# Gate/up weight sums of a seven-product block scheme: made once in DRAM by accumulating DMAs instead of on the chip for every use

## The chip, the cores and the metric

The kernel runs on one core of a Trainium2 chip. A core has a matrix engine (TensorE, PE in the profile), a vector engine (VectorE, DVE), a scalar engine (ScalarE, ACT), a general engine (GpSimd, POOL) and an engine that only issues transfers here (SyncE, SP). Each runs its own list of instructions in order and waits on semaphores that the others, or transfers, raise. Sixteen DMA engines move data between DRAM and the on-chip memory SBUF; PSUM is the memory of eight banks into which TensorE accumulates. The metric is the time of one execution on the device in microseconds.

## The reference

One layer of a decoder: 2048 tokens of width 1024, all float32.

```python
xn = rms_norm(h, mix_norm_w[l])
proj = jnp.einsum('bsd,de->bse', xn, w_in[l])        # 1024 -> 3072: q, f, i, g, lru_x, lru_gate
o_hg = hgrn2_mix(q, f_logit, i_v, g, lb_all[l], hg_norm_w[l])   # gated linear recurrence, 4 heads
o_lru = rglru_mix(lru_x, lru_gate, conv_w[l], ...)              # convolution, gates, linear recurrence
h = h + jnp.einsum('bse,ed->bsd', mixed, w_out[l])
hn = rms_norm(h, ffn_norm_w[l])
gate, up = jnp.split(jnp.einsum('bsd,df->bsf', hn, w_gate_up[l]), 2, axis=-1)   # 1024 -> 2 x 2816
h = h + jnp.einsum('bsf,fd->bsd', jax.nn.silu(gate) * up, w_down[l])
return rms_norm(h, final_norm_w)
```

## The kernel before

**Precision and halves.** Each float32 operand of a large matmul is split into a rounded part `hi` (a cast on ScalarE, L207 or L163) and the remainder `lo` (a subtraction on VectorE, L208 or L164). One product is then three matmuls: hi by hi, lo by hi, hi by lo. The tokens are worked in two halves of 1024, each in two chunks of 512. Both halves go through the projections, the mixers and the output projection first; then come gate/up and down for half 0, then gate/up and down for half 1.

**Start of the program.** For half 0 the first chunk of x is normalised and transposed on the chip (`norm_first`). The second chunk comes already transposed: `xk` (L482) loads one of eight tiles of 128 features, VectorE multiplies it by the norm weight and by a row of inverse norms (L483) that GpSimd and TensorE made (`ss_x`, `dg`, `tpb`, L475 and L476), and it is split into `xn`. The value projection `pv` (L246 to L248) of the four token tiles of chunk 0 comes first, then that of chunk 1, tile by tile of the contraction. After that come eight pairs of feature projections, `pa` and `pb` (L234 to L236), each for both chunks, with the mixers' steps between. Weights arrive as `raw_in` of 512 KB (L161) in three buffers.

**GpSimd's part in the mixers.** GpSimd copies the last three columns of each convolution input into `hist` (L389), which VectorE reads for the next chunk (L387), and raises sums of squares to the power -1/2 in `oss` (L379), which VectorE then multiplies with (L380).

**Gate/up.** Two tiles of 128 weight columns (a11, a12 and a21, a22, by halves of the contraction) and two chunks of tokens (b11 to b22) form a 2 by 2 block product, which seven products P1 to P7 give instead of eight. One such quad is 7 x 12 matmuls of 512 columns; there are 22 quads for each half. `Sums` loads a quad's weights in two DMAs (`raw`), makes the four sums S1 to S4 on VectorE and splits seven operands of 512 columns. The sums of the activations (`act_a` to `act_g`) are made once for each half. In `ffn_up` the products go into four PSUM banks, where P2, P3 and P4 add onto P1, P5 and P7, and five additions on VectorE fold them.

**What sets the order.** The program is written in order of use, but a scheduler decides when it is built where each instruction stands in its engine's list; it lets one overtake another where data and buffers allow. DMAs of one queue share eight completion semaphores in turn: each waits until the one eight places ahead in its queue has landed. SyncE issues every DMA of the kernel before.

Of the kernel before, what the change touches and what calls it, by code (L numbers as in the profile page):

```python
# [8 lines left out]
F32 = mybir.dt.float32  # L9
# [26 lines left out]
def hybrid_layer(ctx: ExitStack, tc: tile.TileContext, x, x_t, norm_w, cols, w_in, gate_w, w_out, w_gu, w_down, out):  # L36
# [467 lines left out]
    def acts(src, nm, direct):  # L504
        ops = {}
        held = []

        def put(name, k, p):
            split([ops[name][s][:, k, :] for s in range(2)], p)

        pages = {}

        def open_(names):
            for name in names:
                ops[name] = [block(f"act_{LET[name]}{s}_{nm}") for s in range(2)]


        def early(k):
            if k == 0:
                open_(("p1", "p5"))  # L520
            b11, b12 = (xin(f"{t}{k}_{nm}") for t in ("b11e_", "b12e_"))
# [3 lines left out]
            tt_(b12, b12, b11, SUB_)  # L525
            put("p5", k, b12)

        def load(k):
            if k == 0:
                open_(("p1", "p5", "p6", "p7", "p2", "p3", "p4") if direct else ("p6", "p7", "p2"))  # L530
            b11, b12 = (xin(f"{t}{k}_{nm}") for t in ("b11_", "b12_"))
            b21, b22 = ((late if direct else page)(f"{t}{k}_{nm}") for t in ("b21_", "b22_"))
            for p, n, c in ((b11, 0, 0), (b12, 0, 1), (b22, 1, 1), (b21, 1, 0)):
                nc.sync.dma_start(out=p, in_=src[n][k, :, c * CW : (c + 1) * CW])
            pages[k] = b11, b12, b21, b22

        def one(k):
            b11, b12, b21, b22 = pages[k]
            if direct:
                put("p1", k, b11)  # L540
            tt_(b11, b12, b11, SUB_)
            if direct:
                put("p5", k, b11)

        def two(k):
            b11, b12, b21, b22 = pages[k]
            tt_(b11, b22, b11, SUB_)
            tt_(b12, b22, b12, SUB_)
            put("p2", k, b21)
            put("p6", k, b11)  # L550
            tt_(b21, b21, b11, SUB_)
            put("p7", k, b12)
            if direct:
                put("p3", k, b22)
                put("p4", k, b21)
            held.append((b22, b21))

        def rest(i):
            name = ("p3", "p4")[i]
# [12 lines left out]
    ORDER = ("p1", "p5", "p6", "p7", "p2", "p3", "p4")  # L572


    class Sums:
        def __init__(self, src, nm):
            self.src, self.nm, self.op, self.raw, self.done = src, nm, {}, [None, None], set()

        def load(self, i):
            r = rawt(f"raw{i}_{self.nm}", (P, 2, CW))  # L580
            nc.sync.dma_start(out=r, in_=self.src[:, :, i * CW : (i + 1) * CW].rearrange("u p k -> p u k"))
            self.raw[i] = r

        def make(self, i):
            (a11, a21), (a12, a22) = ([r[:, u, :] for u in range(2)] if r is not None else (None, None) for r in self.raw)
            nm, name = self.nm, ORDER[i]
            if name == "p1":
                x = a11
            elif name == "p5":
                self.s1 = x = late("s1" + nm)  # L590
                tt_(x, a21, a22, ADD)
            elif name == "p6":
                self.s2 = x = late("s2" + nm)
                tt_(x, self.s1, a11, SUB_)
            elif name == "p7":
                x = late("s3" + nm)
                tt_(x, a11, a21, SUB_)
            elif name == "p2":
                x = a12
            elif name == "p3":  # L600
                x = late("s4" + nm)
                tt_(x, a12, self.s2, SUB_)
            else:
                x = a22
            w = wslot(f"wgu_{LET[name]}_{nm}", (P, 2, CW))
            split([w[:, s, :] for s in range(2)], x)
            self.op[name] = w

    def product(ps, w, b, first):
        for k in range(4):  # L610
            ks = slice(k * P, (k + 1) * P)
            hi, lo = b[0][:, k, :], b[1][:, k, :]
            for n, (s, x) in enumerate(((0, hi), (1, hi), (0, lo))):
                nc.tensor.matmul(  # L614
                    ps, lhsT=w[:, s, ks], rhs=x, start=first and k + n == 0, stop=k == 3 and n == 2, skip_group_check=not first
                )
# [5 lines left out]
    def sums(q):  # L622
        if q < len(quads) and q not in made:
            half, j, m = quads[q]
            f0 = m * NF + 2 * j
            made[q] = Sums(w_gu[f0 : f0 + 2], f"{half}_{j}_{m}")
        return made.get(q)

    def sums_start(q):
        s = sums(q)  # L630
        s.load(0)
        s.load(1)

    def ffn_up(half, bops, between=()):
        between = list(between)
        q0 = half * 2 * NPAIR
        for q in range(q0, q0 + 2 * NPAIR):
            _, j, m = quads[q]
            nm = f"{half}_{j}_{m}"
            s, nxt, nn = sums(q), sums(q + 1), sums(q + 2)  # L640
# [3 lines left out]
            end = q == q0 + 2 * NPAIR - 1 and half == 0  # L644
            for i, name in enumerate(ORDER):
                if q == q0 and i not in s.done:
                    s.make(i)
                product(dst[name], s.op.pop(name), bops[name], i < 4)
                if name == "p1":
                    e1 = page("e1" + nm)  # L650
                    nc.scalar.copy(out=e1, in_=b1)
                elif name == "p5":
                    e5 = page("e5" + nm)
                    nc.scalar.copy(out=e5, in_=b3)
                elif name == "p6":
                    u2 = page("u2" + nm)
                    tt_(u2, e1, b2, ADD)
                elif name == "p7":
                    u3 = page("u3" + nm)
                    tt_(u3, u2, b4, ADD)  # L660
                    tt_(e5, u3, e5, ADD)
                    if m == 0:
                        nc.scalar.activation(out=e5, in_=e5, func=AF.Silu)
                        sg22 = e5
                    else:
                        tt_(e5, e5, sg22, MUL)
                        a22 = e5
                elif name == "p2":
                    if m == 0:
                        sg11 = page("sg11" + nm)  # L670
                        nc.scalar.activation(out=sg11, in_=b1, func=AF.Silu)
                    else:
                        tt_(sg11, sg11, b1, MUL)
                        a11 = sg11
                elif name == "p3":
                    tt_(e1, u2, b3, ADD)
                    if m == 0:
                        nc.scalar.activation(out=e1, in_=e1, func=AF.Silu)
                        sg12 = e1
                    else:  # L680
                        tt_(e1, e1, sg12, MUL)
                        a21 = e1
                else:
                    tt_(u2, u2, b4, ADD)
                    if m == 0:
                        nc.scalar.activation(out=u2, in_=u2, func=AF.Silu)
                        sg21 = u2
                    else:
                        tt_(u2, u2, sg21, MUL)
                        store(half, j, a11, u2, a21, a22)  # L690
                if nxt is not None and not end:
                    nxt.make(i)
                    nxt.done.add(i)
                if between:
                    between.pop(0)()
                if nn is not None and i in (0, 4) and quads[q + 2][0] == half:
                    nn.load(i // 4)
            made.pop(q)


# [236 lines left out]
    for half in range(2):  # L937
# [36 lines left out]
        for s in range(8):  # L974
# [4 lines left out]
            for c in range(NC):  # L979
# [13 lines left out]
                pend.append(nxt)  # L993
        wg = ws.take(4)
# [76 lines left out]
        else:  # L1071
            first = sums(0)
            for i in range(1, 7):
                if i in (3, 5):
                    last.pop(0)()
                first.make(i)
                first.done.add(i)
            sums(1).load(0)
            sums(1).load(1)


    for half in range(2):
        ffn_up(half, bops[half], later if half == 0 else ())
        hp = residual(half)
        if half == 0:
# [5 lines left out]
            def first(i):  # L1091
                if i == 0:
                    sums_start(q)
                sums(q).make(i)
                sums(q).done.add(i)

            for c in range(NC):
                down_plain(0, c, range(16, NF), hp, extra, [lambda i=i: first(i) for i in range(7)] if c == 1 else ())
            fin.clear()
            sums(q + 1).load(0)  # L1100
            sums(q + 1).load(1)
# [7 lines left out]
def _layout(i):  # L1109
# [10 lines left out]
    def by_cols(w):  # L1120
        n = w.shape[1] // P
        return w.reshape(KT, P, n, P).transpose(2, 1, 0, 3).reshape(n, P, D)

# [14 lines left out]
    for m, t in enumerate((a["lru_wa"][0], a["lru_wx"][0])):  # L1138
# [11 lines left out]
        "w_gu": by_cols(a["w_gate_up"][0]),  # L1150
# [21 lines left out]
```

## Time and profile before

Three runs took 2129.33, 2132.01 and 2132.49 us. One execution was profiled.

| | us |
|---|---|
| median of the runs | 2132.01 |
| the profiled execution (its span) | 2131.1 |
| TensorE busy | 2101.2 (99%) |
| VectorE busy | 1493.1 (70%) |
| ScalarE busy | 1010.2 (47%) |
| GpSimd busy | 82.2 (4%) |
| DMA, mean over the span | 123 GB/s |

A group of instructions is told as line, engine, operation, what is written from what, count, busy us, mean ns of one, and the idle time of its engine just before, with what ended it. In a timeline a row begins with the start and the length in us. Numbers of buffers are left out of names. The mean of a pipelined matmul (0.39 us) is its latency; the distance from one to the next is shorter and is read from counts.

### The profile page before, as it was taken

The page shows a single profiled execution, that of the slowest core. Times are in us where ns is not written, and L with a number is a line of the kernel's source. Part 1 is how long each engine was busy: PE and PEld are TensorE (multiplying, and loading weights), DVE is VectorE, ACT ScalarE, POOL GpSimd, SP SyncE. Part 2 cuts the span into 40 slices and gives each one's busy share as a digit, 9 for nine tenths or more (in the row PEclk, how much of TensorE's full clock was granted, in tenths as well). Part 3 has the DMA queues.
Part 4 walks back from the last instruction along what each step waited for, and adds up shares of the span by engine and source line. Part 5 has one row for each costly group of instructions (what it writes and reads, how often), then busy time and mean ns, then how long its engine had stood idle before and what let it go on. Part 6 is the DMA issues. An engine that isn't in the chain of part 4 may idle for free.

```text
span 2131.1 us, 26161 instructions
## 1 busy us (share of the span) xinstructions
PE 2101.2 (99%) x9704; PEld 1735.7 (81%) x9704; DVE 1493.1 (70%) x2415; ACT 1010.2 (47%) x1647; POOL 82.2 (4%) x130
## 2 busy tenths in 40 slices
PE   8999999999999999999999999999999999999998
PEld 6887888888878888788888888888888888888887
DVE  6577664645776566877667669878867667669787
ACT  5577764535777644533333334335433333334333
POOL 2000001100000000000000000000000000000000
PEclk9999999999999999999999999999999999999999
DMA  6111104852111058433323257346423223257424
GB/s 216 61 40 40 40 20 160 282 162 69 31 39 40 20 174 260 156 112 99 106 93 129 89 187 253 109 136 205 143 94 119 95 90 123 94 206 252 156 88 143
DMA packets 138420, 262.84 MB, mean 123 GB/s; under 512 B 11186, under 2 KB 27570, under 8 KB 138292
## 3 DMA queue, kind: packets, MB, share of 16 engines
q1 hardware_dynamic: 138292, 261.17, 36.5%
q8 instruction: 76, 1.25, 0.2%
q14 instruction: 52, 0.43, 0.1%
HBM read 197.95 MB, written 63.18 MB: 123 GB/s over the span
## 4 chain that ended last, share of the span: by engine, by line
PE 83%; ACT 6%; DVE 5%; DMA 3%; issue 2%; SPq 0%; POOL 0%; DVEq 0%; POOLq 0%; ACTq 0%
PE quad_e L614 11%; PE quad_g L614 11%; PE quad_a L614 11%; PE pda L885 10%; PE pdb L885 6%; PE quad_f L614 5%; PE poh L246 2%; PE poh L247 2%; PE poh L248 2%; PE pb L236 2%; PE pb L234 2%; PE pb L235 2%; PE pa L234 1%; PE pa L235 1%; PE pg L248 1%
## 5 line engine op out<-in xcount | busy, mean ns | idle before, releaser
L614 PE MATMUL quad_f<-act_f,wgu_f 128*128 128x512 f32 x528 | 127.4, 389 | 1.8 <-DVE h L1050 1.7
L614 PE MATMUL quad_a<-act_a,wgu_a 128*128 128x512 f32 x528 | 127.5, 389 | 0.0
L614 PE MATMUL quad_g<-act_d,wgu_d 128*128 128x512 f32 x528 | 127.0, 389 | 0.2 <-DVE u L498 0.2
L614 PE MATMUL quad_g<-act_g,wgu_g 128*128 128x512 f32 x528 | 127.1, 390 | 0.0
L614 PE MATMUL quad_a<-act_b,wgu_b 128*128 128x512 f32 x528 | 127.1, 389 | 0.0
L614 PE MATMUL quad_e<-act_e,wgu_e 128*128 128x512 f32 x528 | 127.0, 389 | 0.0
L614 PE MATMUL quad_e<-act_c,wgu_c 128*128 128x512 f32 x528 | 126.9, 389 | 0.0
L614 PEld LDWEIGHTS quad_f<-act_f,wgu_f 128*128 128x128 f32 x528 | 99.0, 188 | 23.1 <-ACT act_g L207 2.1
L498 DVE TENSOR_TENSOR u<-u,quad_g 128x512 f32<-128x512 f32 x88 | 60.5, 687 | 80.9 <-PE quad_g L614 80.9
L614 PEld LDWEIGHTS quad_g<-act_d,wgu_d 128*128 128x128 f32 x528 | 99.0, 188 | 21.1 <-DVE u L498 0.6
L614 PEld LDWEIGHTS quad_e<-act_c,wgu_c 128*128 128x128 f32 x528 | 99.1, 188 | 20.6
L614 PEld LDWEIGHTS quad_g<-act_g,wgu_g 128*128 128x128 f32 x528 | 99.0, 188 | 20.8 <-DVE wgu_g L208 0.3
L614 PEld LDWEIGHTS quad_e<-act_e,wgu_e 128*128 128x128 f32 x528 | 99.0, 188 | 20.6
L614 PEld LDWEIGHTS quad_a<-act_b,wgu_b 128*128 128x128 f32 x528 | 99.0, 188 | 20.5
L614 PEld LDWEIGHTS quad_a<-act_a,wgu_a 128*128 128x128 f32 x528 | 98.9, 188 | 20.6 <-ACT act_c L207 0.2
L234 PE MATMUL pa<-xn,whi_in 128*128 128x512 f32 x256 | 101.7, 397 | 0.0
L236 PE MATMUL pb<-xn,whi_in 128*128 128x512 f32 x256 | 101.0, 395 | 0.0
L235 PE MATMUL pb<-xn,wlo_in 128*128 128x512 f32 x256 | 101.0, 394 | 0.0
L234 PE MATMUL pb<-xn,whi_in 128*128 128x512 f32 x256 | 100.9, 394 | 0.0
L235 PE MATMUL pa<-xn,wlo_in 128*128 128x512 f32 x256 | 100.6, 393 | 0.0
L236 PE MATMUL pa<-xn,whi_in 128*128 128x512 f32 x256 | 100.5, 393 | 0.0
L248 PE MATMUL poh<-whi_o,mx 128*128 128x512 f32 x256 | 99.9, 391 | 0.0
(331 smaller groups left out, 4940.9 us busy)
## 6 DMA issues: line engine op xcount, KB each, us to landing
raw<-in_w_gu SPq DMA_DIRECT2D x88, 512.0 KB, 3.8
raw_in<-in_w_in SPq DMA_DIRECT2D x48, 512.0 KB, 3.5
ao_p<-as SPq DMA_DIRECT2D x76, 256.0 KB, 2.6
raw_o<-in_w_out SPq DMA_DIRECT2D x32, 512.0 KB, 4.4
x<-in_x SPq DMA_DIRECT2D x32, 256.0 KB, 5.8
xrh<-in_x SPq DMA_DIRECT2D x32, 256.0 KB, 3.9
h<-h SPq DMA_DIRECT2D x32, 256.0 KB, 3.5
hn<-hths SPq DMA_DIRECT2D x32, 256.0 KB, 3.3
```

The source lines that it names most:

```text
L234: nc.tensor.matmul(ps, lhsT=whi[:, ks], rhs=hi, start=(k == 0), stop=False)
L235: nc.tensor.matmul(ps, lhsT=wlo[:, ks], rhs=hi, start=False, stop=False)
L236: nc.tensor.matmul(ps, lhsT=whi[:, ks], rhs=lo, start=False, stop=(k == KT - 1))
L246: nc.tensor.matmul(ps, lhsT=hi, rhs=whi[:, ks], start=(k == 0), stop=False)
L247: nc.tensor.matmul(ps, lhsT=hi, rhs=wlo[:, ks], start=False, stop=False)
L248: nc.tensor.matmul(ps, lhsT=lo, rhs=whi[:, ks], start=False, stop=(k == KT - 1))
L498: (e or v).tensor_tensor(out=out, in0=a, in1=b, op=op)
L614: nc.tensor.matmul(ps, lhsT=w[:, s, ks], rhs=x, start=first and k + n == 0, stop=k == 3 and n == 2, skip_group_check=not first)
L885: nc.tensor.matmul(ps, lhsT=x, rhs=y, start=first and q + n == 0, stop=q == gr.n - 1 and n == 2, skip_group_check=not first)
```

## The change

The host lays the gate/up weights out by quads, so that a11, a12, a21 and a22 are four arrays. During the projections of half 0, `combine` makes the four sums in DRAM, for pieces of two quads (512 KB) each: plain copies on SyncE put a21, a11, a11 and a12 into S1, S3, S2 and S4; then accumulating DMAs on GpSimd add a22 to S1 and a21 to S3, S1 to S2, and S2 to S4. That is 44 copies and 44 accumulates. The signs of the scheme are changed to suit (sums only; P6's activations are negated, and two results are negated in the Silu or the multiplication).

In gate/up a quad's seven operands come ready from DRAM in seven loads of 256 KB, two side by side in a buffer, and are split two at a time. P1, P6, P7 and P4 add up in one PSUM bank in that order (P5 and P3 in a second, P2 in a third); the bank is read after each of them, and three additions fold the rest. Matmuls are the same in number and shape.

```diff
+    PIECE = 2
+    NQ = 2 * NPAIR
+    gu_s = [[dram.tile([PIECE, P, CW], F32, name=f"gus{i}_{p}") for p in range(NQ // PIECE)] for i in range(4)]
+
+    def combine(p, step):
+        qs = slice(p * PIECE, (p + 1) * PIECE)
+        a11, a12, a21, a22 = (w_gu[i, qs] for i in range(4))
+        s1, s2, s3, s4 = (gu_s[i][p] for i in range(4))
+        if step == 0:
+            for s, a in ((s1, a21), (s3, a11), (s2, a11), (s4, a12)):
+                nc.sync.dma_start(out=s, in_=a)
+        else:
+            for s, a in (((s1, a22), (s3, a21)), ((s2, s1),), ((s4, s2),))[step - 1]:
+                nc.gpsimd.dma_start(out=s, in_=a, accum_op=ADD, max_dma_last_dim=8192)
+
+    combines = [
+        [lambda p=t - k, k=k: combine(p, k) for k in range(4) if 0 <= t - k < NQ // PIECE] for t in range(NQ // PIECE + 3)
+    ]
...
         def load(self, i):
+            names = ORDER[2 * i : 2 * i + 2]
             r = rawt(f"raw{i}_{self.nm}", (P, 2, CW))
-            nc.sync.dma_start(out=r, in_=self.src[:, :, i * CW : (i + 1) * CW].rearrange("u p k -> p u k"))
+            for u, name in enumerate(names):
+                nc.sync.dma_start(out=r[:, u, :], in_=self.source(name))
             self.raw[i] = r
...
-            w = wslot(f"wgu_{LET[name]}_{nm}", (P, 2, CW))
-            split([w[:, s, :] for s in range(2)], x)
-            self.op[name] = w
+            names = ORDER[2 * i : 2 * i + 2]
+            n = len(names)
+            hi, lo = (wslot(f"wgu{'hl'[z]}{i}_{self.nm}", (P, 2, CW)) for z in range(2))
+            split((hi[:, 0:n, :], lo[:, 0:n, :]), self.raw.pop(i)[:, 0:n, :])
+            for u, name in enumerate(names):
+                self.op[name] = hi[:, u, :], lo[:, u, :]
...
-            b1, b3, b2, b4 = (mk(f"quad_{i}_{nm}") for i in "aefg")
-            dst = dict(p1=b1, p5=b3, p6=b2, p7=b4, p2=b1, p3=b3, p4=b4)
+            ba, bb, bc_ = (mk(f"quad_{i}_{nm}") for i in "abc")
+            dst = dict(p1=ba, p5=bb, p6=ba, p3=bb, p7=ba, p2=bc_, p4=ba)
...
                 elif name == "p6":
-                    u2 = page("u2" + nm)
-                    tt_(u2, e1, b2, ADD)
+                    e2 = page("e2" + nm)
+                    nc.scalar.copy(out=e2, in_=ba)
+                elif name == "p3":
+                    tt_(e2, e2, bb, ADD)
...
                     r = lru_pre(i, pa, pb, nm)
                     nxt = [lambda i=i, r=r, c=c, nm=nm: lru_post(i, *r, ys[c], nm)]
                 pend.append(nxt)
+                if half == 0 and combines:
+                    for f_ in combines.pop(0):
+                        f_()
```

`combines.pop(0)` stands in the loop over feature projections, once for each pair and chunk. Where the scheduler puts the transfers is not to be seen in the diff. SyncE's list before, at the loads of the second chunk (`raw_in` weights, `xk` the tiles of x, the last number a buffer's):

```order
L161 DMA raw_in_5_659<-in_w_in 128x1024
L161 DMA raw_in_6_665<-in_w_in 128x1024
L482 DMA xk_1_0_506<-in_x_t 128x512
L482 DMA xk_1_1_511<-in_x_t 128x512
L482 DMA xk_1_2_516<-in_x_t 128x512
L482 DMA xk_1_3_521<-in_x_t 128x512
L482 DMA xk_1_4_526<-in_x_t 128x512
L482 DMA xk_1_5_531<-in_x_t 128x512
L482 DMA xk_1_6_536<-in_x_t 128x512
L482 DMA xk_1_7_541<-in_x_t 128x512
L161 DMA raw_in_7_671<-in_w_in 128x1024
```

The changed kernel's list at the same loads (`gus` are the sums, by piece and buffer):

```order
L584 DMA gus_9_131<-in_w_gu 16x8192
L584 DMA gus_9_120<-in_w_gu 16x8192
L584 DMA gus_9_142<-in_w_gu 16x8192
L584 DMA gus_10_110<-in_w_gu 16x8192
L584 DMA gus_10_132<-in_w_gu 16x8192
L584 DMA gus_10_121<-in_w_gu 16x8192
L584 DMA gus_10_143<-in_w_gu 16x8192
L482 DMA xk_1_4_570<-in_x_t 128x512
L482 DMA xk_1_5_575<-in_x_t 128x512
L161 DMA raw_in_7_715<-in_w_in 128x1024
L482 DMA xk_1_6_580<-in_x_t 128x512
L482 DMA xk_1_7_585<-in_x_t 128x512
```

The list now has all 44 copies ahead of `xk_1_4`: the first stands behind the gate weights (`graw`) and just ahead of `raw_in_4`, and between the first and the last stand `raw_in_4` to `raw_in_6`, two loads of x and `xk_1_0` to `xk_1_3`. GpSimd's list before, from the last inverse norms of the second chunk to the first mixer steps:

```order
L202 TENSOR_TENSOR ss_x_1_3_353<-ss_x_1_3_353,tinies 128x1
L475 TENSOR_SCALAR dg_1_308<-ident,ss_x_1_3_353 128x128
L389 COPY hist<-xp_1_0_1003 128x3
L379 TENSOR_TENSOR oss_0_0_936<-oss_0_0_936,tinies 128x4
L389 COPY hist<-xp_1_1_1109 128x3
L379 TENSOR_TENSOR oss_0_1_1052<-oss_0_1_1052,tinies 128x4
```

And in the changed kernel, at the last of the accumulating DMAs (each adds one sum onto another):

```order
L587 DMA gus_7_140<-gus_7_118 64x2048
L587 DMA gus_8_141<-gus_8_119 64x2048
L587 DMA gus_9_142<-gus_9_120 64x2048
L587 DMA gus_10_143<-gus_10_121 64x2048
L389 COPY hist<-xp_1_0_1057 128x3
L379 TENSOR_TENSOR oss_0_0_990<-oss_0_0_990,tinies 128x4
L389 COPY hist<-xp_1_1_1170 128x3
L379 TENSOR_TENSOR oss_0_1_1113<-oss_0_1_1113,tinies 128x4
```

All 44 accumulating DMAs now stand ahead of the first `hist`; the first six of them stand among the norms of the first half's tokens (`ss_x`, `dg`).

More of the change, by code (lines that the diff above doesn't have):

```diff
@@ L506, in acts, with put @@
         held = []
-        def put(name, k, p):
-            split([ops[name][s][:, k, :] for s in range(2)], p)
+        def put(name, k, p, scale=None):
+            split([ops[name][s][:, k, :] for s in range(2)], p, scale)
         pages = {}
@@ new lines, in hybrid_layer, with __init__, source @@
+    combines = [
+        [lambda p=t - k, k=k: combine(p, k) for k in range(4) if 0 <= t - k < NQ // PIECE] for t in range(NQ // PIECE + 3)
+    ]
+    class Sums:
+        def __init__(self, q, nm):
+            self.q, self.nm, self.op, self.raw, self.done = q, nm, {}, {}, set()
+        def source(self, name):
+            q = self.q
+            i = {"p1": 0, "p2": 1, "p4": 3}.get(name)
+            if i is not None:
+                return w_gu[i, q]
+            return gu_s[{"p5": 0, "p6": 1, "p7": 2, "p3": 3}[name]][q // PIECE][q % PIECE]
@@ L586, in make @@
[L586 to L604, printed above, removed]
@@ L614, in product @@
                 nc.tensor.matmul(
-                    ps, lhsT=w[:, s, ks], rhs=x, start=first and k + n == 0, stop=k == 3 and n == 2, skip_group_check=not first
+                    ps, lhsT=w[s][:, ks], rhs=x, start=first and k + n == 0, stop=k == 3 and n == 2, skip_group_check=not first
                 )
@@ L630, in sums_start @@
         s = sums(q)
-        s.load(0)
-        s.load(1)
+        for i in range(3):
+            s.load(i)
     def ffn_up(half, bops, between=()):
         between = list(between)
-        q0 = half * 2 * NPAIR
-        for q in range(q0, q0 + 2 * NPAIR):
+        q0 = half * NQ
+        for q in range(q0, q0 + NQ):
             _, j, m = quads[q]
             nm = f"{half}_{j}_{m}"
-            s, nxt, nn = sums(q), sums(q + 1), sums(q + 2)
+            s, nxt = sums(q), sums(q + 1)
             mk = bank if m == 0 else aux
-            b1, b3, b2, b4 = (mk(f"quad_{i}_{nm}") for i in "aefg")
-            dst = dict(p1=b1, p5=b3, p6=b2, p7=b4, p2=b1, p3=b3, p4=b4)
-            end = q == q0 + 2 * NPAIR - 1 and half == 0
+            ba, bb, bc_ = (mk(f"quad_{i}_{nm}") for i in "abc")
+            dst = dict(p1=ba, p5=bb, p6=ba, p3=bb, p7=ba, p2=bc_, p4=ba)
+            stop = q == q0 + NQ - 1
+            end = stop and half == 0
@@ L645, in ffn_up @@
             for i, name in enumerate(ORDER):
-                if q == q0 and i not in s.done:
-                    s.make(i)
-                product(dst[name], s.op.pop(name), bops[name], i < 4)
+                product(dst[name], s.op.pop(name), bops[name], name in ("p1", "p5", "p2"))
                 if name == "p1":
                     e1 = page("e1" + nm)
-                    nc.scalar.copy(out=e1, in_=b1)
+                    nc.scalar.copy(out=e1, in_=ba)
                 elif name == "p5":
@@ L691, in ffn_up @@
-                if nxt is not None and not end:
-                    nxt.make(i)
-                    nxt.done.add(i)
+                        sg21 = page("sg21" + nm)
+                        nc.scalar.activation(out=sg21, in_=ba, func=AF.Silu, scale=-1.0)
+                    else:
+                        v.scalar_tensor_tensor(out=sg21, in0=ba, scalar=-1.0, in1=sg21, op0=MUL, op1=MUL)
+                        store(half, j, a11, sg21, a21, a22)
+                ahead(s, nxt, i, end)
                 if between:
@@ L695, in ffn_up, with ahead @@
                     between.pop(0)()
-                if nn is not None and i in (0, 4) and quads[q + 2][0] == half:
-                    nn.load(i // 4)
             made.pop(q)
+    def ahead(s, nxt, i, end):
+        for t, k in ((s, {0: 1, 2: 2, 3: 3}.get(i)), (None if end else nxt, {5: 0}.get(i))):
+            if t is not None and k is not None and k not in t.done:
+                t.make(k)
+                t.done.add(k)
+        for t, k in ((s, {0: 3}.get(i)), (None if end else nxt, {2: 0, 4: 1, 6: 2}.get(i))):
+            if t is not None and k is not None and k not in t.raw and k not in t.done:
+                t.load(k)
@@ L1072, in hybrid_layer @@
             first = sums(0)
-            for i in range(1, 7):
-                if i in (3, 5):
-                    last.pop(0)()
+            for i in range(1, 3):
                 first.make(i)
                 first.done.add(i)
-            sums(1).load(0)
-            sums(1).load(1)
+                last.pop(0)()
     for half in range(2):
@@ L1093, in first @@
                     sums_start(q)
-                sums(q).make(i)
-                sums(q).done.add(i)
+                else:
+                    sums(q).make(i - 1)
+                    sums(q).done.add(i - 1)
             for c in range(NC):
-                down_plain(0, c, range(16, NF), hp, extra, [lambda i=i: first(i) for i in range(7)] if c == 1 else ())
+                down_plain(0, c, range(16, NF), hp, extra, [lambda i=i: first(i) for i in range(4)] if c == 1 else ())
             fin.clear()
-            sums(q + 1).load(0)
-            sums(q + 1).load(1)
         else:
```

71 lines of the change are left out of this document (32 added, 39 removed).

## The prediction

> **What bounds the kernel now.** I read the page's engine totals first, then the busy time by stretch, then TensorE's waits, and last the timelines of the first 110 us. The page:
>
> ```profile
> span 2131.1 us, 26161 instructions
> PE 2101.2 (99%) x9704; PEld 1735.7 (81%) x9704; DVE 1493.1 (70%) x2415; ACT 1010.2 (47%) x1647; POOL 82.2 (4%) x130
> q1 hardware_dynamic: 138292, 261.17, 36.5%
> ```
>
> TensorE (PE) is idle for 2131.1 - 2101.2 = 29.9 us in all, and every byte moves through one queue that SyncE (SP) issues. By stretch (columns: stretch, PE busy, weight load, DVE, ACT, POOL, granted clock, DMA share, GB/s):
>
> ```profile
> 0.00:16.00 16.00, 9.91 (x27) 5.78 (x28) 7.75 (x11) 7.97 (x14) 5.52 (x24) 1.00 0.85 310
> 16.00:40.00 24.00, 22.68 (x115) 18.68 (x114) 13.44 (x46) 15.56 (x40) 5.74 (x10) 1.00 0.54 189
> 40.00:60.00 20.00, 19.91 (x88) 15.97 (x87) 11.85 (x17) 7.44 (x13) 0.00 (x0) 1.00 0.50 158
> 800.00:900.00 100.00, 97.52 (x451) 78.90 (x450) 74.29 (x119) 51.05 (x99) 5.04 (x6) 1.00 0.66 206
> 1100.00:1200.00 100.00, 100.00 (x442) 82.79 (x442) 67.86 (x102) 34.18 (x58) 0.00 (x0) 1.00 0.29 101
> ```
>
> In the gate/up stage (1100:1200) PE is never idle: 442 matmuls in 100 us, 0.226 us each, at granted clock 1.00. Both programs hold the same matmuls (8750 of 512 columns among them), so neither can get through that stage faster than PE does now. TensorE's waits around the stage's start:
>
> ```profile
> PE quad_f L614 <- DVE h L1050: 1.7, 1, 1.7
> PE tp_hs L222 <- DVE h L1026: 0.4, 2, 0.2
> PE quad_g L614 <- DVE u L498: 0.2, 1, 0.2
> ```
>
> They are 2.3 us, and the idle time of 800:900 is 2.5 us. That is all the change could win. What it can lose is any stall in the projections, because PE has no slack behind it to make one good.
>
> **Part 1: work taken off VectorE and ScalarE.** The groups that it touches (operation, count, then busy us and mean ns):
>
> ```profile
> L498 DVE TENSOR_TENSOR s<-raw,raw 128x512 f32<-128x512 f32 x44 | 30.4, 690 | 33.1 <-DMA raw<-in_w_gu 33.1
> L208 DVE TENSOR_TENSOR wgu_c<-s,wgu_c 128x512 fp32r<-128x512 f32 x44 | 30.4, 692 | 0.6
> L164 DVE TENSOR_TENSOR wlo_in<-raw_in,whi_in 128x1024 fp32r<-128x1024 f32 x48 | 58.6, 1220 | 22.0 <-PE pv L248 7.1 <-PE pb L235 6.3 <-ACT whi_in L163 5.0
> L163 ACT CAST whi_in<-raw_in 128x1024 fp32r<-128x1024 f32 x48 | 50.3, 1047 | 18.8 <-DMA raw_in<-in_w_in 17.4 <-PE pv L248 1.1
> L651 ACT COPY e<-quad_a 128x512 f32<-128x512 f32 x44 | 25.8, 587 | 66.3 <-PE quad_a L614 66.3
> ```
>
> Each quad loses four sums on DVE, 4 x 0.69 = 2.8 us. Its seven splits (7 x 0.69 = 4.8) become three of 1024 columns and one of 512 (3 x 1.22 + 0.69 = 4.4). Five folds of PSUM become three, 2 x 0.69 = 1.4 less. Together 2.8 + 0.4 + 1.4 = 4.6 us of DVE in a quad of 84 x 0.226 = 19.0 us. ScalarE gains one copy (0.59) and saves about as much on wider casts. All of this lies beside a PE that is 100.00 of 100.00 busy, so it is worth 0; the bounds are 0 and 2.5 us.
>
> **Part 2: one PSUM bank for P1, P6, P7, P4.** P6 may enter the bank only when P1 has been copied out, P7 only after the copy of P6, P4 only after DVE has read P7. Between two of them lies at least one product in another bank, 12 x 0.226 = 2.7 us. The longest that ScalarE keeps a copy waiting is one wide cast, 1.05 + 0.59 = 1.64 us. I take 0; without that cover it is up to 44 x (0.59 + 0.59 + 0.69) = 82 us.
>
> **Part 3: 88 DMAs inside DRAM, and where they stand.** This term decides. There are 44 copies of 512 KB on SP and 44 accumulating DMAs of 512 KB on POOL. The source spreads them over the first half's projections, but the scheduled order does not: the copies stand from just ahead of `raw_in_4` up to `xk_1_4`, and all 44 accumulates stand ahead of POOL's first `hist`. What those places are in time (SP, then PE, DVE and POOL):
>
> ```profile
> 15.87 0.33 SPq L161 DMA_DIRECT2D raw_in<-in_w_in  x1
> 25.49 19.13 SPq L482 DMA_DIRECT2D xk<-in_x_t  x8
> 48.62 0.33 SPq L161 DMA_DIRECT2D raw_in<-in_w_in  x1
> ...
> 40.59 0.50 PE L246 MATMUL pv<-whi_in,xn 128*128 128x512 f32 x1
> ...
> 103.17 0.16 DVE L387 COPY xp<-hist 128x3 f32<-128x3 f32 x1
> 103.69 0.69 DVE L380 TENSOR_TENSOR v<-po,oss 128x512 f32<-128x512 f32 x1
> ...
> 33.85 0.61 POOL L475 TENSOR_SCALAR dg<-ident,ss_x 128x128 f32<-128x128 f32 x1
> 94.28 0.45 POOL L389 COPY hist<-xp 128x3 f32<-128x3 f32 x1 [59.82 <-ACT xp L388]
> ```
>
> *Price of a copy.* No DRAM-to-DRAM transfer is in this trace; its 512 KB loads land so (count, KB each, median us from issue to landing):
>
> ```profile
> raw_in<-in_w_in SPq DMA_DIRECT2D x48, 512.0 KB, 3.5
> ```
>
> That is latency, which eight in flight hide; the price is the room taken on the engines. In 0:16 the engines moved 310 GB/s at a share of 0.85, so 365 GB/s when full, and 512 KB (524,288 B) take 1.44 us of all 16 engines. That is the lower bound. The upper is twice that, 2.88 us, if reading and writing the same memory costs both ways. I take 1.44.
>
> *Price of an accumulate.* It reads two operands and writes one: from 1.44 us (no dearer than a load) to three passes, 4.32 us. I take the two reads, 2.88 us. The Trainium skill, "Collectives: The Full Stack", section "Part 3" on why ReduceScatter is half of AllGather, says that a reducing transfer reads two sources through one ring and so halves the rate; no run here shows it yet.
>
> *The wait on SP.* `xk_1_4` feeds the fifth of eight contraction tiles of the second token chunk's value projection. That projection begins at 40.59 us; its first four tiles are 4 x 4 x 3 = 48 matmuls, so the fifth is wanted at 40.59 + 48 x 0.226 = 51.4 us. Between landing and use lie the scaling and the split:
>
> ```profile
> L483 DVE SCALAR_TENSOR_TENSOR xk<-xk,par,tpb x8: 739/741/748, 39.1 to 49.8; 128x512 f32<-128x512 f32 x8
> L207 ACT CAST xn<-xk x8: 620/621/623, 39.9 to 50.5; 128x512 fp32r<-128x512 f32 x8
> L208 DVE TENSOR_TENSOR xn<-xk,xn x8: 683/684/685, 41.8 to 51.6; 128x512 fp32r<-128x512 f32 x8
> ```
>
> 0.74 + 0.62 + 0.68 = 2.0 us, so it must land by 49.4. SP keeps at most eight DMAs in flight, each waiting for the one eight places ahead, so the load cannot pass the copies. From the first copy at 15.9 us: 44 copies, 63.4; the ten loads among them and `xk_1_4` itself (three of 512 KB, seven of 256 KB), 9.4; and the accumulates that run at the same time. Two of a piece's four accumulates need nothing but copies, so I count 22 x 2.88 = 63.4. Landing is at 15.9 + 63.4 + 9.4 + 63.4 = 152.1, which is 102.7 us late. `xk_1_5` to `xk_1_7` with `raw_in_7` between them come 3.6 us later at full rate and some 10 us later beside accumulates; PE has 10.9 us of work on that half, so I add 3 us. Queued behind the late load are the splits of xn, and PE in order behind those.
>
> *The wait on POOL.* All 88 DMAs and the loads around them end at 15.9 + 63.4 + 9.4 + 44 x 2.88 + 9 = 224 us. POOL, with eight in flight, can reach `hist` up to 23 us before that, at 201 to 224. DVE wants `hist` and the power in `oss` at 103.2 + 102.7 = 206. The two waits fall nearly together, so the second adds 0 to 18 us, less some 10 us of matmuls that PE still has ready. I take 0.
>
> Sum: 2131.1 + 102.7 + 3 = 2236.8 us of span. The profiled execution is 2131.1 and the median of the runs 2132.01, 0.9 more, so **2238 us**.
>
> **Against this, from the notes.** The Trainium skill, "DMA: Bandwidth & Descriptors", section "Latency and other measured facts", gives 207 to 214 GB/s each way for copies between HBM tensors; by that figure a copy would be an estimated 2.45 us, 44 of them 108, and the result about 2282 us.
>
> **Rivals.**
>
> *Light.* The accumulates cost no more than loads, 1.44 us. Landing is at 15.9 + 63.4 + 9.4 + 31.7 = 120.4, 71 late, 74 with the restart: 2206 us. If the loads also get ahead of the accumulates, it is 88.7, 39 late, and POOL at some 155 us adds a few: about 2178. For it: a load's price is the only one that the trace has. Against it: an accumulate must read twice.
>
> *Heavy.* Copies at 2.88 and accumulates at 4.32: landing at 15.9 + 126.7 + 9.4 + 95.0 = 247, 198 late, 201 with the restart. Then POOL is free only at 316 to 351 and DVE wants it at 304, which leaves 2 to 37 us after the 10 us of cover: 2335 to 2370 us. For it: both sides of each transfer are the same memory. Against it: at 365 GB/s the engines may be what limits, not the memory.
>
> *Hidden, not slower.* The transfers fit into the room that the DMA engines have (share 0.54 and 0.50 in 16:60), the second chunk's operands are in time, and only part 1 is left: 2129 to 2132 us. This holds if `xk_1_4` lands by 49.4, so if 44 copies take no more than 49.4 - 15.9 - 9.4 = 24.1 us, 0.55 us each, which is 957 GB/s. The best stretch shows 365. Only if SP's loads overtook the copies would it come true.
>
> *The bank turns too slowly.* Part 2 costs up to 82 us on top, decided where ScalarE has two wide casts ahead of a copy (2 x 1.05 + 0.59 = 2.69 us against 2.7). Against it: ScalarE is busy for 34.18 of 100 us in that stage.
>
> **Chances.** The forecast (about 2210 to 2270) 0.44, light 0.21, heavy with the values between (2270 to 2370) 0.25, hidden 0.06, the bank 0.04. The range runs from the cheapest light case to within the heavy one, 2172 to 2345, and leaves out hidden and the top of heavy. What a measurement of this kernel can tell from no change is about 0.2%, 4 us. Only hidden is not slower by more than that; of its 0.06 I give 0.02 to faster and 0.04 to the same, and round slower to 0.94.
>
> **What would show it.** In the changed kernel's first 250 us: a DMA share near 1 from 16 us on; PE idle before `pv` of the second chunk, with `xn` and behind it the DMA `xk` as releaser; POOL's first `hist` at about 200 us and not 94; 512 KB copies whose landing takes many times the 3.5 us of a weight load. From about 400 us on each stage should take what it takes now, with PE at 442 matmuls per 100 us in the gate/up stage. Wrong would be: gaps in the gate/up stage (part 2), PE without a gap before 100 us (hidden), or a stall that starts at `hist` and not at `xn` (the order of the two waits).

## Result and the profile after

The changed kernel takes 2265.35 us (median of four runs, 2263.61 to 2267.75); the kernel before, run beside it, 2132.25 us (2129.33 to 2133.12). The ratio is 1.063, with a 95% interval of 1.0615 to 1.0645: slower by 133 us. Predicted were 2238 us, in a range of 2172 to 2345.

The page of the changed kernel: engine totals, the two queues that move data (packets, MB, share of the 16 engines' span), and the new transfers (count, KB each, median us from issue to landing):

```profile
span 2264.1 us, 26155 instructions
PE 2118.7 (94%) x9704; PEld 1745.2 (77%) x9704; DVE 1302.9 (58%) x2019; ACT 1010.8 (45%) x1560; POOL 118.6 (5%) x174
q1 hardware_dynamic: 160116, 318.86, 41.9%
q0 software_dynamic: 3520, 23.07, 5.1%
gus<-in_w_gu SPq DMA_DIRECT2D x44, 512.0 KB, 20.0
gus<-in_w_gu POOLq DMA_DIRECT2D x22, 512.0 KB, 13.8
gus<-gus POOLq DMA_DIRECT2D x22, 512.0 KB, 20.4
```

VectorE is relieved as planned: 190 us less busy. TensorE (PE) is idle for 2264.1 - 2118.7 = 145.4 us, where it was idle for 29.9. The stretches (columns: stretch, PE, weight load, DVE, ACT, POOL, granted clock, DMA share, GB/s) show where:

```profile
16.00:40.00 24.00, 14.65 (x67) 11.35 (x65) 9.14 (x35) 8.63 (x18) 3.91 (x5) 0.86 1.04 316
40.00:60.00 20.00, 10.26 (x40) 8.40 (x40) 3.50 (x9) 7.28 (x21) 9.31 (x14) 0.67 1.00 311
60.00:200.00 140.00, 50.67 (x171) 38.95 (x172) 20.11 (x29) 18.35 (x26) 27.55 (x35) 0.64 1.03 267
1100.00:1200.00 100.00, 99.31 (x438) 81.91 (x437) 46.47 (x59) 34.40 (x49) 0.00 (x0) 1.00 0.45 150
```

From 16 to 200 us the DMA engines are full and PE works for 75.6 of 184 us. What TensorE waited for, over the whole program (total us, times, longest):

```profile
PE pv L246 <- ACT xn L207: 94.8, 7, 33.7
PE tp_x L222 <- DVE x L448: 14.2, 2, 13.8
PE pk L329 <- DVE lg L315: 10.4, 5, 5.8
PE quad_a L624 <- DVE wgul L208: 6.3, 9, 0.7
```

The first row is the second chunk's value projection, waiting for its operand; the second is the transpose of a tile of x of the first chunk. The timelines of SP, DVE, PE and POOL at that place (in brackets the idle time before, and what ended it):

```profile
98.84 33.61 SPq L584 DMA_DIRECT2D gus<-in_w_gu  x12
134.51 2.67 SPq L482 DMA_DIRECT2D xk<-in_x_t  x2
...
156.74 0.75 DVE L483 SCALAR_TENSOR_TENSOR xk<-xk,par,tpb 128x512 f32<-128x512 f32 x1 [27.90 <-DMA xk<-in_x_t]
...
44.78 1.94 PE L222 MATMUL tp_x<-ident,x 128*128 128x128 f32 x8 [13.83 <-DVE x L448]
...
74.89 0.80 PE L246 MATMUL pv<-whi_in,xn 128*128 128x512 f32 x1 [19.85 <-ACT xn L207]
...
115.65 0.80 PE L246 MATMUL pv<-whi_in,xn 128*128 128x512 f32 x1 [33.66 <-ACT xn L207]
...
158.19 0.80 PE L246 MATMUL pv<-whi_in,xn 128*128 128x512 f32 x1 [28.98 <-ACT xn L207]
...
156.24 0.79 POOL L587 DMA_DIRECT2D gus<-gus  x1 [2.07 <-issue]
197.69 0.79 POOL L587 DMA_DIRECT2D gus<-gus  x1 [2.15 <-issue]
221.33 0.55 POOL L389 COPY hist<-xp 128x3 f32<-128x3 f32 x1 [22.85 <-DVE G L290]
```

`xk_1_4` is issued at 134.5 us, behind all the copies, and lands at 156.7. PE takes it up at 158.2, where 51.4 was wanted: 106.8 us late. PE is starved well before that. The loads that stand among the copies are late too: PE idles 13.8 us for a tile of x, 19.9 us for `xk_1_0`, 33.7 us for `xk_1_2` and 29.0 us for `xk_1_4`. These waits follow one another, so the last load behind the copies sets the total. The first pair of feature projections (`pa`) then begins at 182.9 us:

```profile
L234 PE MATMUL pa<-xn,whi_in x256: 387/389/797, 182.9 to 828.5; 128*128 128x512 f32 x128
```

The same row of the kernel before, and two of its waits that are used below:

```profile
L234 PE MATMUL pa<-xn,whi_in x256: 387/389/797, 62.6 to 700.7; 128*128 128x512 f32 x128
...
PE pk L329 <- DVE lg L315: 6.5, 3, 2.9
PE pd L752 <- DVE hd L498: 0.7, 1, 0.7
```

182.9 - 62.6 = 120.3 of the 133 us are lost before the first feature projection. The first gate/up product (before, then changed) shows where the rest goes:

```profile
L614 PE MATMUL quad_a<-act_a,wgu_a x528: 388/389/478, 849.5 to 1897.5; 128*128 128x512 f32 x176
...
L624 PE MATMUL quad_a<-act_a,wguh x352: 387/389/398, 977.9 to 2027.1; 128*128 128x512 f32 x176
```

Up to there the changed kernel is 977.9 - 849.5 = 128.4 us late, so 8.1 us are lost between `pa` and gate/up. From there to the end it takes 2264.1 - 977.9 = 1286.2 us against 2131.1 - 849.5 = 1281.6, another 4.6.

### The profile page after: what moved, and what is told of

Read it like the earlier page. It is cut to its first block, busy times and chain, and to the rows that moved or that the text cites. A ratio compares the mean times of both kernels' runs of the same rounds, so it can differ in the third digit from the quotient of the medians.

```text
span 2264.1 us, 26155 instructions
## 1 busy us (share of the span) xinstructions
PE 2118.7 (94%) x9704; PEld 1745.2 (77%) x9704; DVE 1302.9 (58%) x2019; ACT 1010.8 (45%) x1560; POOL 118.6 (5%) x174
## 4 chain that ended last, share of the span: by engine, by line
PE 77%; DMA 10%; ACT 7%; DVE 4%; issue 1%; SPq 0%; DVEq 0%; POOLq 0%; POOL 0%; ACTq 0%
PE quad_a L624 21%; PE quad_b L624 10%; PE pda L894 9%; PE pdb L894 7%; PE quad_c L624 5%; DMA gus<-in_w_gu 3%; DMA xk<-in_x_t 3%; PE poh L246 2%; PE poh L248 2%; PE poh L247 2%; DMA raw_in<-in_w_in 2%; PE pg L248 1%; PE pg L246 1%; PE pg L247 1%; PE pb L236 1%; PE pb L235 1%
## 5 line engine op out<-in xcount | busy, mean ns | idle before, releaser
L208 DVE TENSOR_TENSOR wgul<-raw,wguh 128x1024 fp32r<-128x1024 f32 (+1 forms) x176 | 191.9, 1091 | 411.6 <-issue 166.8
L207 ACT CAST wguh<-raw 128x1024 fp32r<-128x1024 f32 (+1 forms) x176 | 166.8, 948 | 298.6 <-PE quad_a L624 174.5
L624 PE MATMUL quad_a<-act_a,wguh 128*128 128x512 f32 x352 | 118.9, 389 | 0.0
L624 PE MATMUL quad_b<-act_e,wguh 128*128 128x512 f32 x352 | 117.4, 389 | 0.0
L624 PE MATMUL quad_a<-act_f,wguh 128*128 128x512 f32 x352 | 115.7, 390 | 0.2 <-ACT e L659 0.2
L624 PE MATMUL quad_a<-act_g,wguh 128*128 128x512 f32 x352 | 115.5, 389 | 0.0
L624 PE MATMUL quad_c<-act_b,wguh 128*128 128x512 f32 x352 | 115.5, 389 | 0.0
L624 PE MATMUL quad_a<-act_d,wguh 128*128 128x512 f32 x352 | 115.5, 389 | 0.0
L624 PE MATMUL quad_b<-act_c,wguh 128*128 128x512 f32 x352 | 115.5, 389 | 0.0
L247 PE MATMUL poh<-wlo_o,mx 128*128 128x512 f32 x256 | 100.1, 394 | 0.5 <-DVE wlo_o L164 0.4
## 6 DMA issues: line engine op xcount, KB each, us to landing
gus<-in_w_gu POOLq DMA_DIRECT2D x22, 512.0 KB, 13.8
```

The costliest lines, as they stand in the source:

```text
L207: nc.scalar.copy(out=dst[0], in_=src)
L208: v.tensor_tensor(out=dst[1], in0=src, in1=f(dst[0]), op=ALU.subtract)
L247: nc.tensor.matmul(ps, lhsT=hi, rhs=wlo[:, ks], start=False, stop=False)
L624: nc.tensor.matmul(ps, lhsT=w[s][:, ks], rhs=x, start=first and k + n == 0, stop=k == 3 and n == 2, skip_group_check=not first)
```

## Experiments

The theory: the loss is the second chunk's loads standing behind copies in SP's queue, and the copies and accumulates share the DMA engines. The rivals: the volume of the transfers costs wherever they stand; POOL's accumulates hold up the mixers; the single PSUM bank turns too slowly. In the edits, `tc.issue_after(m)` orders issue on one engine only: what follows stands behind instruction `m` in that engine's list. Ratios are to the kernel before, run beside each.

**1. The spread of the source, held.** Copies are issued behind the latest weight load of SP at that step, accumulates behind POOL's latest mixer operation.

```diff
-                nc.sync.dma_start(out=s, in_=a)
+                with tc.issue_after(mark["sp"]):
+                    nc.sync.dma_start(out=s, in_=a)
...
-                nc.gpsimd.dma_start(out=s, in_=a, accum_op=ADD, max_dma_last_dim=8192)
+                with tc.issue_after(mark["pool"]):
+                    nc.gpsimd.dma_start(out=s, in_=a, accum_op=ADD, max_dma_last_dim=8192)
```

> The whole change, the same 88 transfers, but the order of issue holds the source's spread: on SP all of the second chunk's xk loads and raw_in_7 stand ahead of the first copy and then eight copies between two weight loads; on POOL the accumulates stand between the mixers' operations. Theory (the loss is the second chunk's operands queued behind copies): PE's wait before pv of the second chunk falls from 29 us to under 3, the projections start near 63 us and not 183, so some 120 us of the 133 come back: 2135 to 2150 us. Rival, the volume of 67 MB through the DMA engines costs wherever it stands: above 2230 us. Rival, POOL's accumulates hold up hist and oss: the stall moves to the first output normalisation, 2170 to 2230 us.

Measured: 2158.02 us, ratio 1.0126 (1.0111 to 1.0141). `pa` begins at 62.9 us and no wait of `pv` for `xn` is left: 107 of the 133 us come back with the same bytes moved. That rules out volume as the main cause. It is 8 us above the range of the theory, and the rest of this trace says why in the main (stretches; VectorE's wait for POOL over the whole program; POOL and DVE around 200 us):

```profile
60.00:100.00 40.00, 37.50 (x178) 30.77 (x177) 18.60 (x49) 22.69 (x30) 1.06 (x3) 0.96 1.02 335
100.00:200.00 100.00, 88.60 (x456) 72.53 (x454) 59.01 (x135) 60.50 (x106) 28.43 (x36) 0.96 0.99 258
...
DVE v L381 <- POOL oss L380: 18.9, 6, 9.6
...
198.07 0.79 POOL L590 DMA_DIRECT2D gus<-gus  x1 [4.62 <-issue]
198.61 1.32 POOL L380 TENSOR_TENSOR oss<-oss,tinies 128x4 f32<-128x4 f32 x1
199.97 0.69 DVE L381 TENSOR_TENSOR v<-po,oss 128x512 f32<-128x512 f32 x1 [9.62 <-POOL oss L380]
201.31 0.80 PE L414 MATMUL pr<-xl,gw 128*128 128x512 f32 x1 [7.80 <-DVE xl L209]
```

The DMA engines are still full from 60 to 200 us. POOL cannot issue an accumulate until one eight places ahead has landed and the sums that it works on are there; `oss` stands behind it in POOL's list, VectorE behind `oss`, and PE behind VectorE. So the rival on POOL is true of most of what is left here, though not of the changed kernel. Late weights have a part in it: ScalarE waited 6.2 and 4.7 us for `raw_in` before 91 us, and 2.5 us of PE's idle time, at 96 us, come behind the second of these waits.

**2. No transfers inside DRAM.** P5, P6, P7 and P3 read plain weight blocks; the sums are left out.

```diff
-            return gu_s[{"p5": 0, "p6": 1, "p7": 2, "p3": 3}[name]][q // PIECE][q % PIECE]
+            return w_gu[{"p5": 2, "p6": 0, "p7": 0, "p3": 1}[name], q]
...
-                if half == 0 and combines:
-                    for f_ in combines.pop(0):
-                        f_()
```

> The 88 transfers are left out, and the products P5, P6, P7 and P3 read plain weight blocks where the change reads sums (so the sums are missing from the output); everything else in the gate/up part is the change's. Theory (parts 1 and 2 are worth nothing but the nine waits for a buffer of the weight splits, 6.3 us): 2130 to 2140 us, and those nine waits of PE for DVE stay. Rival, one bank for P1, P6, P7, P4 turns too slowly: PE waits for ACT e at many of the 44 quads and the time is 2145 to 2214 us. Rival, the folds and sums saved on VectorE are worth something: 2126 us or less.

Measured: 2136.23 us, ratio 1.0025 (1.0015 to 1.0035). All but some 6 us of the loss is gone, and with it the rival of the slow bank: over 44 quads PE waits 1.1 us for copies out of it. The nine waits for `wgul` stay:

```profile
PE quad_a L624 <- DVE wgul L208: 6.2, 9, 0.7
PE quad_a L624 <- ACT e L659: 1.1, 1, 1.1
...
1100.00:1200.00 100.00, 98.61 (x434) 81.05 (x433) 44.02 (x54) 32.86 (x46) 0.00 (x0) 1.00 0.40 133
```

**3. Copies without accumulates.** The 44 accumulates are left out, so each sum holds one operand.

```diff
-                nc.gpsimd.dma_start(out=s, in_=a, accum_op=ADD, max_dma_last_dim=8192)
+                pass
```

> The 44 accumulates on POOL are left out (so the sums hold one operand only); the 44 copies on SP stay where the change has them. Theory (xk_1_4 lands behind 44 copies of 1.44 to 1.54 us): landing at 15.9 + 44 x 1.5 + 9.4 = 91 us and not 156, PE's restart 40 to 45 us late and not 107, first mixers near 105 to 115 us and not 183: 2185 to 2200 us. Rival, the copies cost the 2.45 us of the notes and the accumulates the rest: landing at 133, about 2230 us. Rival, only the accumulates hurt: under 2145 us. Rival, the copies alone block and the accumulates are hidden beside them: 2255 us or more.

Measured: 2188.22 us, ratio 1.0269 (1.0248 to 1.0289), in the theory's range. SP and PE at the same place:

```profile
87.69 2.13 SPq L482 DMA_DIRECT2D xk<-in_x_t  x2
...
100.67 0.80 PE L246 MATMUL pv<-whi_in,xn 128*128 128x512 f32 x1 [13.85 <-ACT xn L207]
...
L234 PE MATMUL pa<-xn,whi_in x256: 387/389/796, 113.5 to 752.8; 128*128 128x512 f32 x128
```

PE goes on at 100.7 us, 49.3 late, against 106.8 with the accumulates. So the copies make 49.3 us of the stall, and the accumulates 158.19 - 100.67 = 57.5. From `pv` to `pa` it takes 113.5 - 100.7 = 12.8 us, against 182.9 - 158.2 = 24.7 with accumulates beside the last loads.

**4. The same lump, a little later.** The copies stand right behind `raw_in_7` and `xk_1_7`.

```diff
-                nc.sync.dma_start(out=s, in_=a)
+                with tc.issue_after(mark["w7"]), tc.issue_after(mark["xk0"]):
+                    nc.sync.dma_start(out=s, in_=a)
```

> The whole change with all 88 transfers in one lump, but the copies stand right behind xk_1_7 and raw_in_7 of SP's queue, not ahead of them. Theory (place in the queue decides, not volume): the second chunk is on time, no stall before 63 us; the next load in the lump's shadow is raw_in_9 to raw_in_11, wanted between some 75 and 100 us and landing between 90 and 150, so a stall of 30 to 70 us comes there: 2165 to 2210 us. Rival, volume or contention for the memory decides: 2250 us or more. Rival, POOL's accumulates ahead of hist decide: the stall begins at the first output normalisation with hist or oss as releaser.

Measured: 2204.99 us, ratio 1.0347 (1.0327 to 1.0368). The second chunk is in time, and the next loads of SP's queue are late (SP, ScalarE's casts of the weights, PE):

```profile
94.19 0.34 SPq L161 DMA_DIRECT2D raw_in<-in_w_in  x1
101.91 58.99 SPq L586 DMA_DIRECT2D gus<-in_w_gu  x21
173.49 118.24 SPq L161 DMA_DIRECT2D raw_in<-in_w_in  x11
...
118.24 1.04 ACT L163 CAST whi_in<-raw_in 128x1024 fp32r<-128x1024 f32 x1 [16.75 <-DMA raw_in<-in_w_in]
207.48 1.04 ACT L163 CAST whi_in<-raw_in 128x1024 fp32r<-128x1024 f32 x1 [32.70 <-DMA raw_in<-in_w_in]
...
208.58 0.79 PE L235 MATMUL pb<-xn,whi_in 128*128 128x512 f32 x1 [30.93 <-ACT whi_in L163]
```

The same 88 transfers cost 60 us less than in the changed kernel, and the stall has moved to whatever load stands behind them: weights from `raw_in_9` on in place of `xk`. The place in the queue sets which load is late, and how much. The built order is not quite the same lump: three weight loads stand among the copies, and on POOL some of the mixers' operations now stand among the accumulates (the first `hist` at 113.6 us). PE's larger waits here are 5.8, 8.4, 9.7 and 30.9 us. Before the two middle ones ScalarE had waited for weights; a wait of VectorE for `oss`, 2.5 us, lies in the 9.7.

**5. One buffer for P4.** The change takes a two-operand buffer each for `hi` and `lo` of P4, which is a single operand: eight buffers for a quad, of nine. In the changed kernel's trace VectorE waits for such a buffer, which P4's product still reads, and PE then for VectorE:

```profile
1162.55 1.22 DVE L208 TENSOR_TENSOR wgul<-raw,wguh 128x1024 fp32r<-128x1024 f32 x1 [4.75 <-PE quad_a L624]
...
1163.83 0.50 PE L624 MATMUL quad_a<-act_a,wgul 128*128 128x512 f32 x1 [0.69 <-DVE wgul L208]
```

This run is experiment 2 (no transfers, sums left out) with both parts of P4 in one buffer.

```diff
-            hi, lo = (wslot(f"wgu{'hl'[z]}{i}_{self.nm}", (P, 2, CW)) for z in range(2))
+            if n == 1:
+                w = wslot(f"wguh{i}_{self.nm}", (P, 2, CW))
+                hi, lo = w[:, 0:1, :], w[:, 1:2, :]
+            else:
+                hi, lo = (wslot(f"wgu{'hl'[z]}{i}_{self.nm}", (P, 2, CW)) for z in range(2))
```

> As the run without transfers inside DRAM (2136.2 us; sums missing from the output), but the single product P4 keeps its two splits in one two-operand buffer, where the change gives each of them a buffer of its own and leaves half of it empty: seven buffers of nine in use for a quad and not eight. Theory (the nine waits of quad_a for wgul, 6.2 us, are waits for such a buffer): those nine waits disappear and the time is 2129 to 2132 us. Rival, the waits come from the pace of VectorE's splits or of the loads: they stay, 2135 to 2138 us. Rival, the work taken off VectorE is worth something once the waits are gone: 2127 us or less.

Measured: 2126.74 us, ratio 0.9977 (0.9968 to 0.9986). The nine waits are gone, and the stage is dense again:

```profile
1100.00:1200.00 100.00, 100.00 (x443) 82.81 (x442) 44.46 (x55) 33.41 (x47) 0.00 (x0) 1.00 0.42 143
```

The nine waits cost more than their 6.2 us. In 1100:1200 experiment 2 lacks 9 matmuls of 443, which is 2.0 us, for 100.00 - 98.61 = 1.39 us of idle time (the first matmul after a wait is also slower, 0.50 us above against 0.39). By that ratio nine waits are about 9 us, and the two spans differ by 2133.4 - 2125.0 = 8.4. The theory on the buffer holds, though not its range of 2129 to 2132 us. The result lies just under the 2127 that was the last rival's bound: with the waits gone, the program is 4.5 us faster than before, and most of that lies in the gate/up part (table behind experiment 7).

**6. Half the density, and one buffer for P4.** All transfers, a piece started in every second step of both halves' projections, order held.

```diff
-        [lambda p=t - k, k=k: combine(p, k) for k in range(4) if 0 <= t - k < NQ // PIECE] for t in range(NQ // PIECE + 3)
+        [lambda p=(t - 2 * k) // 2, k=k: combine(p, k) for k in range(4) if t % 2 == 0 and 0 <= t - 2 * k < 2 * (NQ // PIECE)]
+        for t in range(2 * (NQ // PIECE) + 5)
...
-                if half == 0 and combines:
+                if combines:
```

> The whole change with its 88 transfers, one piece (four copies and its four accumulates) started in every second step of both halves' projections and not in every step of the first half's, its steps two apart, the order of issue held; and P4's splits in one buffer. Theory (what is left of the loss with the spread held, 27 us, is a DMA share of 1.00 between 60 and 200 us, with weight loads late behind the transfers; at half the density the share stays at 0.3 to 0.7): 2129 to 2137 us, no stall over 3 us before 300 us. Rival, each transfer costs by itself wherever it stands (waits of POOL's mixer operations behind accumulates): 2145 to 2160 us, as with the denser spread. Rival, the change is a gain once its transfers are hidden: under 2126 us.

Measured: 2128.67 us, ratio 0.9989 (0.9980 to 0.9998). This is 0.3 us under the theory's range, and the reason that I gave was right only in part: the denser spread had lost more to POOL's `oss` than to late weights. Here:

```profile
100.00:200.00 100.00, 99.44 (x500) 82.15 (x497) 68.55 (x146) 75.27 (x121) 18.96 (x22) 1.00 0.56 155
...
DVE v L381 <- POOL oss L380: 2.5, 4, 0.7
```

With all 88 transfers in it, this is some 2.5 us faster than the kernel before. That is less than the 0.2% that I took for what can be told from no change.

**7. Copies and accumulates apart.** Copies at the dense pace in the first half's projections, accumulates at the same pace in the second half's; one buffer for P4.

```diff
-        [lambda p=t - k, k=k: combine(p, k) for k in range(4) if 0 <= t - k < NQ // PIECE] for t in range(NQ // PIECE + 3)
+        [lambda p=t - 16 * (k > 0) - k, k=k: combine(p, k) for k in range(4) if 0 <= t - 16 * (k > 0) - k < NQ // PIECE]
+        for t in range(NQ // PIECE + 19)
```

> The whole change, but copies and accumulates never run together: the 44 copies at the dense spread's pace (four at each of eleven steps) in the first half's projections, the 44 accumulates at the same pace in the second half's, order of issue held, P4's splits in one buffer. In the dense spread DVE waited 17.7 us for POOL's oss, which stood behind accumulates, at a DMA share of 1.00. Theory (POOL is held only because copies and accumulates together, 4 x 1.54 + 4 x 2.62 = 16.6 us a step beside the loads, fill the engines so that eight accumulates in flight don't drain): alone the copies take 6.2 us of a step and the accumulates 10.5, neither fills a step of some 25 us, no wait for oss over 2 us, 2127 to 2133 us. Rival, the accumulates hold POOL by their own chain (each waits for the one whose sum it reads), whatever else the engines do: the waits for oss come back in the second half's projections, 2138 to 2150 us.

Measured: 2130.72 us, ratio 0.9996 (0.9986 to 1.0006). The accumulates' stage and VectorE's wait for `oss`:

```profile
500.00:600.00 100.00, 99.42 (x534) 82.65 (x533) 70.11 (x165) 69.45 (x119) 31.36 (x39) 1.00 0.74 167
...
DVE v L381 <- POOL oss L380: 2.3, 4, 0.7
```

At a DMA share of 0.74 the accumulates drain and POOL is free in time, chain or no chain. So in these runs POOL held up VectorE only where copies and accumulates together filled the engines.

**From the first gate/up product to the end, in each trace.** This stretch holds what the change does to gate/up, apart from the transfers (us; its start is the first `quad_a<-act_a`):

| run | start | to the end |
|---|---|---|
| kernel before | 849.5 | 1281.6 |
| changed kernel | 977.9 | 1286.2 |
| 2, no transfers | 847.0 | 1286.4 |
| 5, no transfers, one buffer for P4 | 847.1 | 1277.9 |
| 6, half the density, one buffer for P4 | 848.8 | 1277.6 |
| 7, copies and accumulates apart, one buffer for P4 | 846.6 | 1277.4 |

The second buffer for P4 costs about 8.5 us, and without it the new gate/up part is about 4 us faster than the one before, with the transfers or without.

## Why the prediction was right, point by point

**The bound.** Right that PE sets the end. But the sum counted only idle time. Of the 133 us, 145.4 - 29.9 = 115.5 are idle time of PE; the other 2118.7 - 2101.2 = 17.5 are a longer busy time for the same 9704 instructions, which I had at nothing (last section). Part of it lies between the waits of the stall, where the next late load sets the time anyway; behind the last one it adds to the loss.

**Part 3, the wait on SP.** Right in mechanism, and nearly in size: 106.8 us against 102.7. I had PE fed until `xk_1_4` was wanted, where the loads among the copies were late as well; since the last load sets the total, this does not change the sum. That the size came out so near is in part luck, for two prices were off, in opposite directions. The *price of a copy* was too low. Experiment 3 has the stall from copies alone: 49.3 us against the 39.3 of my sum (15.9 + 63.4 + 9.4 = 88.7, wanted at 49.4). If the ten loads keep their 9.4 us, the 44 copies took 73.4, so 1.67 us each and not 1.44. The packet time of SyncE's queue gives less: its share in experiment 3 over that in experiment 2, which has no copies, is (43.9% of 2187.9 - 41.8% of 2133.4) / 44 = 1.56 us. By that only half of the 10 us is the copies' price, and the rest is not shown. Either is far from the upper bound of 2.88. The Trainium skill's figure ("DMA: Bandwidth & Descriptors", section "Latency and other measured facts"), by which I had an estimated 2.45 us and 2282 us in all, is too high for these copies: this trace does not agree with it. The page has it for tiles of another shape, 128 partitions of 16 KiB. The *price of an accumulate* was too high. The issue at 156.24 is POOL's thirtieth accumulate, so at least 22 had landed by then, as I had counted. If those 22 made the 57.5 us, they took 2.61 us each and not 2.88; the queue's own share gives the same, 5.1% of 2264.1 us over 44 = 2.62. The Trainium skill's rule that a reducing transfer halves the rate ("Collectives: The Full Stack", "Part 3") is borne out in direction; here the factor is 1.6 to 1.7 (2.61 to 1.67, or 2.62 to 1.56 by the queues' shares).

**Part 3, the restart.** This is the step that was wrong by most. I gave 3 us for `xk_1_5` to `xk_1_7`; it was 24.7 us from `pv` to `pa` instead of 62.6 - 51.4 = 11.2, so 13.5 more. I counted 10 us for these loads, but with accumulates beside them `xk_1_6` was taken up 16 us after `xk_1_4`:

```profile
163.36 0.50 PE L246 MATMUL pv<-whi_in,xn 128*128 128x512 f32 x1
...
174.44 0.80 PE L246 MATMUL pv<-whi_in,xn 128*128 128x512 f32 x1 [8.09 <-ACT xn L207]
```

8.1 us of the 13.5 are this wait. Most of the rest is slow matmuls: the twelve of `xk_1_4` took from 158.19 to 163.36, 5.2 us in place of 12 x 0.226 = 2.7, and the twelve from 174.44 again 5.3. Without accumulates (experiment 3) the restart cost 12.8 - 11.2 = 1.6 us.

**Part 3, the wait on POOL.** Right at 0, with more room than I had: POOL issued its last accumulate at 197.7 us and was then idle for 22.9 us, and the first `hist` at 221.3 waited for DVE. I had the two waits nearly together; the restart, longer than forecast, made part of the room. In experiment 1, in another order of POOL's list, a wait for POOL does appear.

**Part 1, worth 0 to 2.5 us.** The bound was too low. VectorE lost 190 us of work, and with one buffer for P4 and no transfers the gain was 4.5 us (experiment 5; interval 3.0 to 6.8), of which the trace has 1281.6 - 1277.9 = 3.7 from the first gate/up product on. PE's waits of before for `h`, `u` and `hd` (1.7 + 0.4 + 0.2 + 0.7 = 3.0 us) are gone from that trace, and 1.3 us of waits for the bank have come. The remaining 2 us or so are busy time: PE takes 1269.2 us for the 5613 matmuls of this stretch, where it took 1270.9. The bound counted the waits and not the slower matmuls behind them.

**Part 2, taken as 0.** Right on the bank: PE waited 1.3 us for it at most (experiment 5). But I looked only at PSUM and not at the SBUF buffers of the splits. Eight buffers of nine in use for a quad cost some 8 us, the clearest thing I had left out; the prediction's sign that gaps in the gate/up stage would show part 2 wrong would have pointed at the wrong buffers.

**The sum.** Stall 106.8, restart 13.5, then 8.1 between `pa` and gate/up and 4.6 in gate/up (some 8.5 for the buffers less some 4 of gain): 133 us, of which I had 106. Of the 8.1, 3.9 are longer waits of PE for `pk` (10.4 against 6.5); why the mixers ran less smoothly is not shown.

**The rivals.** Light would have needed accumulates at 1.44 us, heavy copies at 2.88; the measured prices lie between. Hidden came true only in experiments 6 and 7, where the queue's order was changed. *The bank* was nowhere seen.

## What to carry to other kernels

Work that is written spread out over a loop and depends on nothing may be pulled together by a scheduler to the first place where its queue is free; look at each queue's list, and ask what is queued behind it. Here the same 88 transfers cost 129 us in the scheduler's order, 69 behind the next loads and 22 with the source's spread held (each against experiment 2, which has none of them), and 2 to 4 us when spread thinner or kept apart (against experiment 5), depending on what they stand ahead of and how many run at once. When operands are paired into wider buffers, count the buffers that a stage holds at its fullest, and the single operand left over.

## What the runs showed of the hardware

After each long stall PE started slow: from 158.19 to 163.36 us `pv` matmuls followed each other every 0.43 us where the dense stage has 0.226. This lasted for 3 to 5 us each time, and the granted clock of the starved stretch was 0.64. A starved TensorE thus pays twice: 2.5 us at this restart, and over the program PE is busy for 17.5 us longer with the same instructions.

A 512 KB copy within DRAM took 1.56 to 1.67 us of the full engines, some tenth more than the 1.44 us estimated for a load of its size, though it is read and written in the same memory. An accumulate took 2.6 us. On landing times the queue matters more than either: 20 us for a copy in the lump, at eight in flight.
